# Attention scores in pairs of query tiles, with the last of five passes on half of the tensor engine's rows

## The chip, the cores and the metric

The kernel runs on one core of one Trainium2 chip. The metric is the device time in microseconds (us) of one execution, from the launch on the chip to its end; lower is better. "PE" is TensorE's matmul stream and "PEld" its weight loads, "DVE" is VectorE, "ACT" ScalarE, "POOL" GpSimd and "SP" SyncE, whose queue issues nearly all DMAs.

## The reference: what is computed

A sequence of 1024 tokens of width 1024 passes through two layers and a final RMSNorm. Layer 0 is causal attention with low-rank q and kv projections, layer 1 a gated convolution. The change touches layer 0 only, and in it the scores of the 8 heads:

```python
q_nope, q_pe = jnp.split(q, [QK_NOPE], axis=-1)       # 128 and 64 wide per head
k_nope, v = jnp.split(kv, [QK_NOPE], axis=-1)
q_pe = apply_rope(q_pe, cos[:, :, None, :], sin[:, :, None, :])
k_pe = apply_rope(k_pe, cos, sin)                     # one k_pe, shared by all heads
q = jnp.concatenate([q_nope, q_pe], axis=-1)
...
s = jnp.einsum('bqhd,bkhd->bhqk', qi, kf) * scale     # + causal mask, softmax, times v
```

A score is thus a sum over 128 plain and 64 rotary channels.

## The kernel before, in words

All matmuls that matter here run on operands of the 32-bit format fp32r, which holds fewer mantissa bits than fp32. Each operand is therefore split into a rounded part (suffix h) and the rest (suffix l), and a product takes several passes that add into the same PSUM tile: high x high, high x low, low x high.

The attention stage runs head by head. `proj(h)` loads the head's rotary part `rq` by four DMAs and its gate, and makes `qh`, `ql`, `kh`, `kl` (tiles `pj`) and, every second head, the values (`pv`). `score(h, i)` makes the scores of query tile i (128 queries) against all keys up to it, in chunks of 256 to 512 columns, in a PSUM tile `S`; there are two such tiles in rotation. Each chunk takes five passes (lines 538 to 542): three over the 128 plain channels, and two with `rq` as weights over the rotary channels. `rq` holds 128 rows: the two 32-row halves of the rounded rotary q (kinds 0 and 1), and below them the two halves of its rest (kinds 2 and 3). `krh` and `krl` hold the rotary k's rounded part and rest, each of them twice, in rows 0 to 63 and again in rows 64 to 127. So the fourth pass (`krh`) adds high x high and low x high at once, and the fifth (`krl`) adds high x low, and low x low. After the five passes the mask is added and the row maximum taken on DVE (lines 545, 546), the exponential on ACT (548), and the division by the row sum on POOL (551); this gives the tile `P`. `attend(h, c)` transposes `P` on PE (tiles `T`, line 564), splits it on ACT and DVE (`pth`, `ptl`) and multiplies with the values into `po`.

The order in which instructions stand on each engine in this stage is set by a scheduler at build time, which goes by the order of the program text as a priority, by free tiles, and by its own estimate of times. On the chip each engine runs its instructions in that order. The first part of the program (up to about 182 us) has a PE order written out by hand.

Of the kernel before, what the change touches and what calls it, by code (L numbers as in the profile page):

```python
# [9 lines left out]
F32 = mybir.dt.float32  # L10
# [3 lines left out]
AF = mybir.ActivationFunctionType  # L14
ALU = mybir.AluOpType
AX = mybir.AxisListType
PSUM = bass.MemoryType.PSUM

P = 128
T = 1024  # L20
# [5 lines left out]
CH = 512  # L26
# [38 lines left out]
def hybrid_body(ctx, tc, xT, xP, pos, cols, w1a, w1b, wqr, wqk, wv, wo, wc, we, out):  # L65
    nc = tc.nc
    v, s, g, pe, sp = nc.vector, nc.scalar, nc.gpsimd, nc.tensor, nc.sync
# [18 lines left out]
    for a in range(1, 4):  # L86
# [4 lines left out]
    ropeS = [[tc.dram_tile([P, T], F32, name=f"ropeS{k}{p_}") for p_ in range(2)]  # L91
             for k in range(4)]
# [5 lines left out]
    def load_w(src, n, nm, alloc=None, eng=None):  # L98
        if alloc is None:
            def alloc(name):  # L100
                return wp.tile([P, 1024], F32R, tag="w", bufs=5, name=name)
        raw = wp.tile([P, 1024], F32, tag="wraw", name=f"wr_{nm}")
        sp.dma_start(raw[:, :n], src)
        hi = alloc(f"wh_{nm}")
        s.activation(hi[:, :n], raw[:, :n], AF.Copy)
        lo = alloc(f"wl_{nm}")
        (eng or early_eng[0]).tensor_tensor(lo[:, :n], raw[:, :n], hi[:, :n].bitcast(F32), ALU.subtract)  # L107
        return hi, lo
# [4 lines left out]
    def split_early(src, nm):  # L113
        raw = wp.tile([P, 1024], F32, tag="wraw", name=f"sr_{nm}")
        sp.dma_start(raw, src)
        hi = wp.tile([P, 1024], F32R, tag="w", bufs=5, name=f"sh_{nm}")
        lo = wp.tile([P, 1024], F32R, tag="w", bufs=5, name=f"sl_{nm}")
        for a in range(2):
            cs = sl(a, CH)
            s.activation(hi[:, cs], raw[:, cs], AF.Copy)  # L120
            early_eng[0].tensor_tensor(lo[:, cs], raw[:, cs], hi[:, cs].bitcast(F32), ALU.subtract)
        loS[nm] = tc.dram_tile([P, 1024], F32, name=f"loS{nm}")
        sp.dma_start(loS[nm], lo.bitcast(F32))
# [13 lines left out]
    def mm3(ps, wh, wl, xh, xl, start, stop):  # L137
        pe.matmul(ps, wh, xh, start=start, stop=False)  # L138
        pe.matmul(ps, wh, xl, start=False, stop=False)  # L139
        pe.matmul(ps, wl, xh, start=False, stop=stop)  # L140
# [67 lines left out]
    def sl(k, n=P):  # L208
        return slice(k * n, (k + 1) * n)
# [9 lines left out]
    krh = midk.tile([P, T], F32R, name="krh")  # L219
    krl = midk.tile([P, T], F32R, name="krl")  # L220
# [187 lines left out]
    for a in range(4):  # L408
        b = a ^ 1
# [51 lines left out]
    b1 = es_b.enter_context(tc.tile_pool(name="b1", bufs=1, reuse_waits="tile"))  # L461
    psS_p = es_b.enter_context(tc.tile_pool(name="psS", bufs=2, space=PSUM, reuse_waits="tile"))
# [3 lines left out]
    mask = b1.tile([P, P], F32, name="mask")  # L466
# [8 lines left out]

    def proj(h):
        rq = b2.tile([P, T], F32R, tag="rq", name=f"rq{h}")
        for kind in range(4):
            sp.dma_start(rq[32 * kind : 32 * kind + 32, :].bitcast(F32),
                         ropeS[kind][h // 4][32 * (h % 4) : 32 * (h % 4) + 32, :])  # L480
        gt = b2.tile([P, T], F32, tag="gate", name=f"gateB{h}")
        sp.dma_start(gt, gateS[h])
        wh, wl = load_w(wqk[h], 640, f"qk{h}")
        q_h = b2.tile([P, T], F32R, tag="qh", name=f"qh{h}")
        q_l = b2.tile([P, T], F32R, tag="ql", name=f"ql{h}")
        k_h = b2.tile([P, T], F32R, tag="kh", name=f"kh{h}")
        k_l = b2.tile([P, T], F32R, tag="kl", name=f"kl{h}")
        for dst_h, dst_l, sh_, sl_, n, off, scale in (
            (q_h, q_l, qnh, qnl, NQL, 0, QSCALE),
            (k_h, k_l, kvh, kvl, NKV, NQL, 1.0),  # L490
        ):
            for c in range(2):
                ch = sl(c, CH)
                ps = psA_p.tile([P, CH], F32, tag="acc", name=f"pj{h}{off}{c}")
                for k in range(n):
                    mm3(ps, wh[:, sl(off + k)], wl[:, sl(off + k)], sh_[k][:, ch], sl_[k][:, ch],
                        k == 0, k == n - 1)
                s.activation(dst_h[:, ch], ps, AF.Copy, scale=scale)
                v.scalar_tensor_tensor(dst_l[:, ch], ps, scale, dst_h[:, ch].bitcast(F32),
                                       ALU.mult, ALU.subtract)  # L500
        if h % 2 == 0:
            wh, wl = load_w(wv[h // 2], 512, f"v{h}")
            vh = b2.tile([P, KD, 256], F32R, tag="vh", name=f"vh{h}")
            vl = b2.tile([P, KD, 256], F32R, tag="vl", name=f"vl{h}")
            for t2 in range(KD // 2):
                ps = psA_p.tile([P, CH], F32, tag="acc", name=f"pv{h}{t2}")
                for a in range(2):
                    tk = sl(2 * t2 + a)
                    for k in range(NKV):
                        pa_ = ps[:, sl(a, 256)]  # L510
                        w_h, w_l = wh[:, sl(k, 256)], wl[:, sl(k, 256)]
                        pe.matmul(pa_, kvh[k][:, tk], w_h, start=(k == 0), stop=False)
                        pe.matmul(pa_, kvl[k][:, tk], w_h, start=False, stop=False)
                        pe.matmul(pa_, kvh[k][:, tk], w_l, start=False, stop=(k == NKV - 1))
                dh = vh[:, 2 * t2 : 2 * t2 + 2, :].rearrange("p a b -> p (a b)")
                dl = vl[:, 2 * t2 : 2 * t2 + 2, :].rearrange("p a b -> p (a b)")
                s.activation(dh, ps, AF.Copy)
                v.tensor_tensor(dl, ps, dh.bitcast(F32), ALU.subtract)
            vpair[h // 2] = (vh, vl)
        heads[h] = (q_h, q_l, k_h, k_l, rq, gt)  # L520

    probs = {}

    def score(h, i):
        q_h, q_l, k_h, k_l, rq, _ = heads[h]
        nk = (i + 1) * P
        ps = psS_p.tile([P, T], F32, tag="S", name=f"S{h}_{i}")
        if i == 0:
            chunks, off = [(0, 256)], 0
        elif i == 4:  # L530
            chunks, off = [(0, 384), (384, 640)], 128
        else:
            chunks, off = [(a, min(a + CH, nk)) for a in range(0, nk, CH)], 0
        qs = sl(i)
        for a, b in chunks:
            o_ = ps[:, off + a : off + b]
            ks = slice(a, b)
            pe.matmul(o_, q_h[:, qs], k_h[:, ks], start=True, stop=False)
            pe.matmul(o_, q_h[:, qs], k_l[:, ks], start=False, stop=False)
            pe.matmul(o_, q_l[:, qs], k_h[:, ks], start=False, stop=False)  # L540
            pe.matmul(o_, rq[:, qs], krh[:, ks], start=False, stop=False)
            pe.matmul(o_, rq[:, qs], krl[:, ks], start=False, stop=True)
        st = b1.tile([P, 3], F32, tag="st", bufs=8, name=f"st{h}_{i}")
        last = ps[:, off + i * P : off + nk]
        v.tensor_tensor(last, last, mask, ALU.add)
        v.tensor_reduce(st[:, 0:1], ps[:, off : off + nk], AX.X, ALU.max, negate=True)  # L546
        pr = b1.tile([P, nk], F32, tag=f"P{i}", bufs=2 if i in (2, 3) else 1, name=f"P{h}_{i}")
        s.activation(pr[:, :nk], ps[:, off : off + nk], AF.Exp, bias=st[:, 0:1],  # L548
                     accum_out=st[:, 1:2])
        v.reciprocal(st[:, 2:3], st[:, 1:2])  # L550
        g.tensor_scalar(pr[:, :nk], pr[:, :nk], st[:, 2:3], 1.0, ALU.mult, ALU.mult)  # L551
        probs[h, i] = pr

    def attend(h, c, dst=None):
        vh, vl = vpair[h // 2]
# [48 lines left out]

    ogt = {}
    proj(0)
    pending = None
    for h in range(NH):
        for i in range(8):
            score(h, i)  # L610
            if i == 1 and pending is not None:
                attend(*pending)
                pending = None
            if i == 3 and h + 1 < NH:
                proj(h + 1)
            if i == 4 and h < 2:
                split_early(wc[22 + h], f"cg{6 + h}")
            if i == 6:
                split_early(we[h], f"e{h}")
            if i == 5:  # L620
                if h < NH - 1:
                    attend(h, 0)
                else:
                    ogt[0] = [load_og("A", h_, 0) for h_ in range(NH - 1)]
                    ogt[0].append(act_tile("A", f"og0{h}"))
                    attend(h, 0, ogt[0][h])
        pending = (h, 1)
# [499 lines left out]
```

## Time and profile before

| what | value |
|---|---|
| time, median of 3 runs | 908.65 us (908.37 to 911.29) |
| profiled execution | 909.12 us, of which span from first to last instruction 907.2 us |
| PE busy | 894.3 us (99%) of the span, 4432 matmuls |
| PEld, DVE, ACT, POOL busy | 82%, 72%, 56%, 41% |
| attention stage | about 182 to 424 us of the span |

The span is what the profiler saw between the first and the last instruction; the profiled execution's own time is 1.92 us longer. A busy PE is one that has at least one matmul on its way; since matmuls are pipelined, what one matmul costs is the distance from its start to the next one's start, not its recorded duration.

### The profile page before, as it was taken

The page shows a single profiled execution, that of the slowest core. Times are in us where ns is not written, and L with a number is a line of the kernel's source. Part 1 is how long each engine was busy: PE and PEld are TensorE (multiplying, and loading weights), DVE is VectorE, ACT ScalarE, POOL GpSimd, SP SyncE. Part 2 cuts the span into 40 slices and gives each one's busy share as a digit, 9 for nine tenths or more (in the row PEclk, how much of TensorE's full clock was granted, in tenths as well). Part 3 has the DMA queues.
Part 4 walks back from the last instruction along what each step waited for, and adds up shares of the span by engine and source line. Part 5 has one row for each costly group of instructions (what it writes and reads, how often), then busy time and mean ns, then how long its engine had stood idle before and what let it go on. Part 6 is the DMA issues. An engine that isn't in the chain of part 4 may idle for free.

```text
span 907.2 us, 12407 instructions
## 1 busy us (share of the span) xinstructions
PE 894.3 (99%) x4432; PEld 745.0 (82%) x4432; DVE 650.4 (72%) x1108; ACT 504.4 (56%) x839; POOL 370.6 (41%) x335
## 2 busy tenths in 40 slices
PE   9999999999999999999999999999999999999996
PEld 7888888888888988978887878888888887778996
DVE  7668957647656666676464958999999997687543
ACT  8435454255555554574343447766666773678732
POOL 0000000143442532642234559999999993000034
PEclk9999999999999999999999999999999999999998
DMA  7223644563332331551364411111112223145714
GB/s 269 93 71 128 221 159 167 224 200 117 121 107 85 120 106 49 185 179 54 111 232 127 154 57 47 48 47 46 47 48 95 93 92 109 54 139 186 267 60 145
DMA packets 39677, 110.18 MB, mean 121 GB/s; under 512 B 5248, under 2 KB 8320, under 8 KB 39616
## 3 DMA queue, kind: packets, MB, share of 16 engines
q1 hardware_dynamic: 39248, 108.74, 36.0%
q8 instruction: 35, 0.57, 0.3%
q10 hardware_dynamic: 288, 0.39, 0.1%
q14 instruction: 26, 0.21, 0.1%
q0 software_dynamic: 80, 0.26, 0.1%
HBM read 83.93 MB, written 24.92 MB: 120 GB/s over the span
## 4 chain that ended last, share of the span: by engine, by line
PE 90%; DMA 3%; DVE 2%; ACT 2%; POOL 1%; issue 1%; SPq 1%; DVEq 0%; ACTq 0%; POOLq 0%
PE ps_b L138 5%; PE ps_b L140 5%; PE ps_b L139 5%; PE cb L139 3%; PE cb L140 3%; PE cb L138 3%; PE cg L138 3%; PE cg L139 3%; PE cg L140 3%; PE e L138 3%; PE e L140 3%; PE e L139 3%; PE T L564 3%; PE ca L138 3%; PE ca L140 3%; PE ca L139 3%
## 5 line engine op out<-in xcount | busy, mean ns | idle before, releaser
L816 POOL TENSOR_TENSOR dcv<-dcv,pkb 128x512 f32<-128x512 f32 (+1 forms) x126 | 157.8, 1255 | 8.5 <-ACT pkb L815 1.0
L815 ACT ACTIVATE pkb<-u,taps 128x512 f32<-128x512 f32 (+1 forms) x126 | 83.6, 674 | 55.9 <-POOL dcv L816 51.2
L551 POOL TENSOR_SCALAR P<-P,st 128x128 f32<-128x128 f32 (+3 forms) x64 | 48.1, 753 | 121.9 <-DVE st L550 114.4
L827 DVE SCALAR_TENSOR_TENSOR av<-u,taps,av 128x512 f32<-128x512 f32 (+1 forms) x135 | 91.8, 688 | 1.2 <-ACT av L821 1.1
L107 POOL TENSOR_TENSOR wl_qk<-wr_qk,wh_qk 128x640 fp32r<-128x640 f32 x8 | 12.6, 1571 | 174.3 <-PE ps_b L139 167.7
L829 DVE SCALAR_TENSOR_TENSOR cv<-su,gsum,cv 128x512 f32<-128x512 f32 (+1 forms) x117 | 80.6, 689 | 0.4
L574 DVE TENSOR_TENSOR ptl<-T,pth 128x512 fp32r<-128x512 f32 (+1 forms) x96 | 52.3, 554 | 30.9 <-ACT pth L573 30.5
L573 ACT ACTIVATE pth<-T 128x512 fp32r<-128x512 f32 (+1 forms) x96 | 46.0, 490 | 50.5 <-PE T L564 44.1
L138 PE MATMUL ps_b<-xgh,wh_b 128*128 128x512 f32 x176 | 69.9, 397 | 0.0
L140 PE MATMUL ps_b<-xgh,wl_b 128*128 128x512 f32 x176 | 69.6, 395 | 0.0
L139 PE MATMUL ps_b<-xgl,wh_b 128*128 128x512 f32 x176 | 69.6, 395 | 0.0
L1006 POOL TENSOR_TENSOR x<-x,rbe 128x512 f32<-128x512 f32 (+1 forms) x16 | 16.2, 1045 | 126.7 <-DMA rbe<-rowe 121.5
L107 POOL TENSOR_TENSOR wl_o<-wr_o,wh_o 128x1024 fp32r<-128x1024 f32 x16 | 41.5, 2596 | 55.4 <-PE o L140 21.8
L138 PE MATMUL e<-a_y,wh_e 128*128 128x256 f32 (+1 forms) x192 | 61.7, 322 | 0.0
L140 PE MATMUL e<-a_y,wl_e 128*128 128x256 f32 (+1 forms) x192 | 61.5, 320 | 0.0
L139 PE MATMUL e<-a_y,wh_e 128*128 128x256 f32 (+1 forms) x192 | 61.4, 320 | 0.0
L548 ACT ACTIVATE P<-S,st 128x128 f32<-128x128 f32 (+3 forms) x64 | 47.4, 741 | 24.2 <-DVE st L546 17.6
L138 PE MATMUL cg<-a_h,wh_cg 128*128 128x512 f32 x128 | 51.7, 404 | 0.0
L139 PE MATMUL cb<-a_h,wh_cb 128*128 128x512 f32 x128 | 50.8, 397 | 0.8 <-DVE a_h L746 0.8
L140 PE MATMUL o<-a_og,wl_o 128*128 128x512 f32 x128 | 51.0, 398 | 0.3 <-POOL wl_o L107 0.3
L138 PE MATMUL o<-a_og,wh_o 128*128 128x512 f32 x128 | 51.0, 400 | 0.1
L138 PE MATMUL ca<-a_h,wh_ca 128*128 128x512 f32 x128 | 50.8, 397 | 0.0
(321 smaller groups left out, 2679.8 us busy)
## 6 DMA issues: line engine op xcount, KB each, us to landing
wr_o<-in_wo_dram SPq DMA_DIRECT2D x16, 512.0 KB, 4.0
wr_e<-in_we_dram SPq DMA_DIRECT2D x14, 512.0 KB, 4.7
wl_e<-loSe SPq DMA_DIRECT2D x14, 512.0 KB, 4.0
wr_b<-in_w1b_dram SPq DMA_DIRECT2D x11, 512.0 KB, 3.3
sr_cg<-in_wc_dram SPq DMA_DIRECT2D x8, 512.0 KB, 4.5
loScg<-sl_cg SPq DMA_DIRECT2D x8, 512.0 KB, 2.9
gateS<-gt SPq DMA_DIRECT2D x8, 512.0 KB, 4.7
rq<-ropeS SPq DMA_DIRECT2D x32, 128.0 KB, 3.4
```

Source lines behind the costliest of these rows:

```text
L107: (eng or early_eng[0]).tensor_tensor(lo[:, :n], raw[:, :n], hi[:, :n].bitcast(F32), ALU.subtract)
L138: pe.matmul(ps, wh, xh, start=start, stop=False)
L139: pe.matmul(ps, wh, xl, start=False, stop=False)
L140: pe.matmul(ps, wl, xh, start=False, stop=stop)
L548: s.activation(pr[:, :nk], ps[:, off : off + nk], AF.Exp, bias=st[:, 0:1], accum_out=st[:, 1:2])
L551: g.tensor_scalar(pr[:, :nk], pr[:, :nk], st[:, 2:3], 1.0, ALU.mult, ALU.mult)
L573: s.activation(hi[:, n0:], pt[:, n0:], AF.Copy)
L574: v.tensor_tensor(lo[:, n0:], pt[:, n0:], hi[:, n0:].bitcast(F32), ALU.subtract)
L815: s.activation(pk, lag(src, i), AF.Copy, scale=tap(of, i))
L816: g.tensor_tensor(acc, acc, pk, ALU.add)
L827: v.scalar_tensor_tensor(a_, lag(E, i), tap(dwe, i), a_, ALU.mult, ALU.add)
L829: v.scalar_tensor_tensor(c_, lag(su, i), tap(gsum, i), c_, ALU.mult, ALU.add)
```

## The change

`score(h, i)` becomes `score_pair(h, i0)`, which is called for every even i and writes two score tiles. For each of the two tiles it writes passes one to four of all chunks; then come the fifth passes of both tiles, chunk by chunk in turn; then the softmax of both. The fifth pass uses 64 rows instead of 128: rows 0 to 63 for even query tiles and rows 64 to 127 for odd ones (`tile_position=(r0, 0)`), so that the two passes of a pair stand in different halves of the array. For this the rounded rotary q must lie in the upper rows for even query tiles and in the lower rows for odd ones: each of the four DMAs of `rq` is cut in two, one for the even and one for the odd blocks of 128 tokens, with the kinds turned by two for the odd ones. The fifth pass now adds high x low alone; the product low x low is left out.

```diff
     def proj(h):
         rq = b2.tile([P, T], F32R, tag="rq", name=f"rq{h}")
+
+        def alt(ap, b):
+            return ap.rearrange("p (i b n) -> p i b n", b=2, n=P)[:, :, b, :]
+
         for kind in range(4):
-            sp.dma_start(rq[32 * kind : 32 * kind + 32, :].bitcast(F32),
-                         ropeS[kind][h // 4][32 * (h % 4) : 32 * (h % 4) + 32, :])
+            for b in range(2):
+                at = 32 * ((kind + 2 * b) % 4)
+                sp.dma_start(alt(rq[at : at + 32, :].bitcast(F32), b),
+                             alt(ropeS[kind][h // 4][32 * (h % 4) : 32 * (h % 4) + 32, :], b))
...
-    def score(h, i):
+    def score_pair(h, i0):
         q_h, q_l, k_h, k_l, rq, _ = heads[h]
...
+        pss, todo = {}, {}
+        for i in (i0, i0 + 1):
...
+            for a, b in chunks:
+                o_ = ps[:, off + a : off + b]
+                ks = slice(a, b)
+                pe.matmul(o_, q_h[:, qs], k_h[:, ks], start=True, stop=False)
+                pe.matmul(o_, q_h[:, qs], k_l[:, ks], start=False, stop=False)
+                pe.matmul(o_, q_l[:, qs], k_h[:, ks], start=False, stop=False)
+                pe.matmul(o_, rq[:, qs], krh[:, ks], start=False, stop=False)
+                todo[i].append((o_, qs, ks))
+            pss[i] = ps, off, nk
+
+        for j in range(max(len(x_) for x_ in todo.values())):
+            for i in (i0, i0 + 1):
+                if j < len(todo[i]):
+                    o_, qs, ks = todo[i][j]
+                    r0 = 64 * (i % 2)
+                    pe.matmul(o_, rq[r0 : r0 + 64, qs], krl[r0 : r0 + 64, ks],
+                              start=False, stop=True, tile_position=(r0, 0))
...
         for i in range(8):
-            score(h, i)
+            if i % 2 == 0:
+                score_pair(h, i)
```

The scheduler turns this text into an order. Three places show what it makes of it. The first is PE in head 0, at the pair of tiles 2 and 3 (`S_2`, `S_3`; line 542 before and line 559 after are the fifth pass; `pv` and `T` are other work). Before:

```order
L538 MATMUL S_2_1660<-kh_1522,qh_1520 128x384
L539 MATMUL S_2_1660<-kl_1523,qh_1520 128x384
L540 MATMUL S_2_1660<-kh_1522,ql_1521 128x384
L541 MATMUL S_2_1660<-krh,rq_1507 128x384
L542 MATMUL S_2_1660<-krl,rq_1507 128x384
L564 MATMUL T_1792<-ident,P_0_1643 128x128
L538 MATMUL S_3_1673<-kh_1522,qh_1520 128x512
L539 MATMUL S_3_1673<-kl_1523,qh_1520 128x512
L540 MATMUL S_3_1673<-kh_1522,ql_1521 128x512
L541 MATMUL S_3_1673<-krh,rq_1507 128x512
L542 MATMUL S_3_1673<-krl,rq_1507 128x512
```

After the change:

```order
L547 MATMUL S_2_1664<-kh_1526,qh_1524 128x384
L548 MATMUL S_2_1664<-kl_1527,qh_1524 128x384
L549 MATMUL S_2_1664<-kh_1526,ql_1525 128x384
L550 MATMUL S_2_1664<-krh,rq_1507 128x384
L559 MATMUL S_2_1664<-krl,rq_1507 128x384
L584 MATMUL T_1800<-ident,P_0_1653 128x128
L547 MATMUL S_3_1669<-kh_1526,qh_1524 128x512
L548 MATMUL S_3_1669<-kl_1527,qh_1524 128x512
L549 MATMUL S_3_1669<-kh_1526,ql_1525 128x512
L550 MATMUL S_3_1669<-krh,rq_1507 128x512
L559 MATMUL S_3_1669<-krl,rq_1507 128x512
```

Nothing moved here: a transpose and four full passes stand between the fifth pass of tile 2 and that of tile 3. The second place is PE in head 4, at tiles 4 and 5, one of the few where the fifth passes of two tiles became neighbours (`po` is the product with the values). Before:

```order
L541 MATMUL S_4_3249<-krh,rq_2785 128x256
L542 MATMUL S_4_3249<-krl,rq_2785 128x256
L538 MATMUL S_5_3267<-kh_2800,qh_2798 128x512
L539 MATMUL S_5_3267<-kl_2801,qh_2798 128x512
L540 MATMUL S_5_3267<-kh_2800,ql_2799 128x512
L541 MATMUL S_5_3267<-krh,rq_2785 128x512
L542 MATMUL S_5_3267<-krl,rq_2785 128x512
```

After the change:

```order
L550 MATMUL S_5_3282<-krh,rq_2801 128x256
L559 MATMUL S_4_3273<-krl,rq_2801 128x384
L559 MATMUL S_5_3282<-krl,rq_2801 128x512
L559 MATMUL S_4_3273<-krl,rq_2801 128x256
L138 MATMUL po_3088<-pth_3094,vh_2110 128x512
L559 MATMUL S_5_3282<-krl,rq_2801 128x256
L139 MATMUL po_3088<-ptl_3095,vh_2110 128x512
```

Here three fifth passes follow each other in alternating halves, and a fourth stands alone. Over the whole program the 96 fifth passes stand in 63 groups of neighbours with other work between the groups; in 4 of the groups passes of both halves meet, and the others hold one pass, or two of the same tile and so of the same half. The third place is the SP queue at the start of the stage, where `rq` of head 0 is loaded. Before:

```order
L479 DMA rq_1507<-ropeS_81 32x1024
L479 DMA rq_1507<-ropeS_83 32x1024
L479 DMA rq_1507<-ropeS_85 32x1024
L479 DMA rq_1507<-ropeS_87 32x1024
L482 DMA gateB_1512<-gateS_89 128x1024
```

After the change:

```order
L485 DMA rq_1507<-ropeS_81 32x4x128 x2
L485 DMA rq_1507<-ropeS_83 32x4x128 x2
L485 DMA rq_1507<-ropeS_85 32x4x128 x2
L485 DMA rq_1507<-ropeS_87 32x4x128 x2
L488 DMA gateB_1516<-gateS_89 128x1024
```

Four issues of 32 rows of 4 KB became eight of 32 rows of four 512-byte pieces, ahead of the gate's load.

## Rows read from the trace of the kernel before

**Rows 1.** The page: busy time of each engine, and PE's granted clock in 40 slices.

```profile
PE 894.3 (99%) x4432; PEld 745.0 (82%) x4432; DVE 650.4 (72%) x1108; ACT 504.4 (56%) x839; POOL 370.6 (41%) x335
...
PEclk9999999999999999999999999999999999999998
```

**Rows 2.** Busy time by stage, in us; the middle stretch is the attention stage.

```profile
182.00:424.00 242.00, 240.43 (x1402) 209.57 (x1401) 155.27 (x341) 136.81 (x298) 95.00 (x124) 1.00 0.39 124
```

**Rows 3.** PE's waits from 182 to 425 us: total, times, longest.

```profile
PE po L139 <- DVE ptl L574: 0.9, 3, 0.5
PE S L538 <- ACT P L548: 0.3, 1, 0.3
PE S L541 <- DMA rq<-ropeS: 0.2, 1, 0.2
```

**Rows 4.** Groups by line and shape: the fifth pass, busy us and mean ns.

```profile
L542 PE MATMUL S<-krl,rq 128*128 128x512 f32 x40 | 16.0, 400 | 0.0
...
L542 PE MATMUL S<-krl,rq 128*128 128x256 f32 x32 | 9.0, 281 | 0.0
...
L542 PE MATMUL S<-krl,rq 128*128 128x384 f32 x24 | 8.1, 336 | 0.0
```

**Rows 5.** Timeline, head 7: start, duration in us; passes and their weight loads.

```profile
413.91 0.40 PE L542 MATMUL S<-krl,rq 128*128 128x512 f32 x1
413.91 0.19 PEld L538 LDWEIGHTS S<-kh,qh 128*128 128x128 f32 x1
414.14 0.28 PE L538 MATMUL S<-kh,qh 128*128 128x256 f32 x1
414.15 0.19 PEld L539 LDWEIGHTS S<-kl,qh 128*128 128x128 f32 x1
414.26 0.28 PE L539 MATMUL S<-kl,qh 128*128 128x256 f32 x1
```

**Rows 6.** Timeline, head 7: passes of 384 columns.

```profile
407.00 0.33 PE L541 MATMUL S<-krh,rq 128*128 128x384 f32 x1
407.00 0.19 PEld L542 LDWEIGHTS S<-krl,rq 128*128 128x128 f32 x1
...
407.17 0.34 PE L542 MATMUL S<-krl,rq 128*128 128x384 f32 x1
```

**Rows 7.** Timeline, head 0: a pass whose weights were loaded late.

```profile
185.93 0.19 PEld L138 LDWEIGHTS pj<-kvh,wh_qk 128*128 128x128 f32 x1 [0.45 <-DVE ql L499]
185.93 0.51 PE L138 MATMUL pj<-kvh,wh_qk 128*128 128x512 f32 x1
...
186.28 0.39 PE L139 MATMUL pj<-kvl,wh_qk 128*128 128x512 f32 x1
```

**Rows 8.** Timeline, head 7: a change from transposes to matmuls.

```profile
412.08 0.39 PE L140 MATMUL po<-pth,vl 128*128 128x512 f32 x1
...
412.31 0.60 PE L564 MATMUL T<-ident,P 128*128 128x128 f32 x4
...
412.64 0.19 PEld L138 LDWEIGHTS po<-pth,vh 128*128 128x128 f32 x1
412.67 0.48 PE L138 MATMUL po<-pth,vh 128*128 128x512 f32 x1
...
412.99 0.39 PE L538 MATMUL S<-kh,qh 128*128 128x512 f32 x1
```

**Rows 9.** Timeline of the SP queue, heads 0 and 1: DMA issues.

```profile
182.53 2.81 SPq L479 DMA_DIRECT2D rq<-ropeS  x4
185.39 0.42 SPq L482 DMA_DIRECT2D gateB<-gateS  x1
```

**Rows 10.** The tile rq: its issues in ns, its way to landing.

```profile
L479 SPq DMA_DIRECT2D rq<-ropeS x32: 302/416/1580, 182.5 to 367.2; - x32
...
DMA to landing us min/median/max: 2.1/3.4/6.1
```

**Rows 11.** Timeline of PE, head 0: the first pass that reads rq.

```profile
189.68 0.36 PE L541 MATMUL S<-krh,rq 128*128 128x256 f32 x1 [0.17 <-DMA rq<-ropeS]
```

**Rows 12.** DVE's waits from 182 to 424 us: total, times, longest.

```profile
DVE st L550 <- ACT P L548: 20.3, 30, 2.8
DVE S L545 <- PE S L542: 19.8, 25, 2.1
DVE ptl L574 <- ACT pth L573: 16.8, 34, 1.6
```

More of the change, by code (lines that the diff above doesn't have):

```diff
@@ L522, in hybrid_body @@
     probs = {}
-    def score(h, i):
+    def score_pair(h, i0):
         q_h, q_l, k_h, k_l, rq, _ = heads[h]
[L526 to L552, printed above, removed]
@@ new lines, in score_pair @@
+        pss, todo = {}, {}
+        for i in (i0, i0 + 1):
+            nk = (i + 1) * P
+            ps = psS_p.tile([P, T], F32, tag="S", name=f"S{h}_{i}")
+            if i == 0:
+                chunks, off = [(0, 256)], 0
+            elif i == 4:
+                chunks, off = [(0, 384), (384, 640)], 128
+            else:
+                chunks, off = [(a, min(a + CH, nk)) for a in range(0, nk, CH)], 0
+            qs = sl(i)
+            todo[i] = []
+            for a, b in chunks:
[7 more added lines that the diff above has]
+            pss[i] = ps, off, nk
@@ new lines, in score_pair @@
+        for j in range(max(len(x_) for x_ in todo.values())):
[5 more added lines that the diff above has]
+                              start=False, stop=True, tile_position=(r0, 0))
+        for i in (i0, i0 + 1):
+            ps, off, nk = pss[i]
+            st = b1.tile([P, 3], F32, tag="st", bufs=8, name=f"st{h}_{i}")
+            last = ps[:, off + i * P : off + nk]
+            v.tensor_tensor(last, last, mask, ALU.add)
+            v.tensor_reduce(st[:, 0:1], ps[:, off : off + nk], AX.X, ALU.max, negate=True)
+            pr = b1.tile([P, nk], F32, tag=f"P{i}", bufs=2 if i in (2, 3) else 1, name=f"P{h}_{i}")
+            s.activation(pr[:, :nk], ps[:, off : off + nk], AF.Exp, bias=st[:, 0:1],
+                         accum_out=st[:, 1:2])
+            v.reciprocal(st[:, 2:3], st[:, 1:2])
+            g.tensor_scalar(pr[:, :nk], pr[:, :nk], st[:, 2:3], 1.0, ALU.mult, ALU.mult)
+            probs[h, i] = pr
```

## The prediction, made before the changed kernel had run

> **What bounds the kernel now.** I read the page first: PE is busy for 894.3 of 907.2 us, the next engine for 72%, and the granted clock is at its upper level (2.4 GHz) in every slice [rows 1]. So the program is as long as PE's row of matmuls. Next the table by stage: the change lies in the attention stage, where PE is busy for 240.4 of 242.0 us with the clock at 1.00 [rows 2]. Third, PE's waits there: 0.9, 0.3 and 0.2 us, 1.4 us together [rows 3]. Two things follow. Nothing that the change does on other engines can give more than these 1.4 us. And whatever it adds to or takes from PE's row comes out in the time one to one.
>
> The unit is then the distance between the starts of neighbouring passes. It is 0.23 us for 512 columns and 0.12 for 256 [rows 5], and 0.17 for 384 [rows 6]; the recorded 0.40, 0.28 and 0.34 hold a tail of about 0.165 us in which the next pass is already running. The reader should also see when weights are loaded: the load of the next pass starts with the pass before it (413.91 and 413.91, 414.14 and 414.15) [rows 5]. So a load costs nothing as long as it may run beside a pass.
>
> **The change part by part.** *What it is worth if two fifth passes share the array.* There are 40, 24 and 32 fifth passes of 512, 384 and 256 columns [rows 4]. At the distances above that is 9.2 + 4.1 + 3.8 = 17.1 us of PE's row. Each head has six pairs of partners; the shorter of each has 256 columns twice, 384 three times, 512 once: 0.24 + 0.52 + 0.23 = 0.98 us a head, 7.9 us in all. That is the most that running side by side can give.
>
> *What the order leaves of it.* PE runs in the order shown in the section on the change. A full pass needs all rows, so only fifth passes that are neighbours can overlap. Of 48 pairs, 5 stand so (three borders of 256 columns, two of 384): 3 x 0.12 + 2 x 0.17 = 0.7 us. The reason is visible at tiles 2 and 3: the second tile waits for its PSUM buffer or its turn, and the scheduler puts the first tile's fifth pass where it stood before. I take -0.7 us, bounds 0 and -0.7.
>
> *What it adds: changes of the array's shape.* The 96 fifth passes stand in 63 groups with 128-row work on both sides. So PE goes 126 times between 128-row and 64-row passes; before, never. No row of the trace before shows such a change, so I bound its price. From below: nothing. The nearest row for that is the change from transposes to matmuls: four transposes start at 412.31, the matmul at 412.67, the one after at 412.99 [rows 8]. The fourth transpose's own start is about 0.03 us ahead of the matmul, so the two together last about 0.35 us, against 0.11 + 0.23 = 0.34 for the same pieces apart (a transpose takes 0.11: four of them between 412.31 and 412.67, less that 0.03). That change of mode is nearly free. But it leaves all 128 rows in one piece. From above: the old pass must leave the array entirely, its tail of 0.165 us, and only then are the new weights loaded, unhidden. An unhidden load has a row: the pass at 185.93 starts with its load instead of after it, lasts 0.51 instead of 0.39, and holds the next start off by 0.35 instead of 0.23 us, 0.12 more [rows 7]; after transposes a late load costs 0.48 against 0.39 or 0.32 against 0.23, 0.09 more [rows 8]. The upper bound is 0.165 + 0.12 = 0.285 us a change.
>
> Between 0 and 0.285 I take 0.12: a load for rows in another grouping cannot run beside a pass that uses them all, but the pass itself needs no more than its columns to get out of the way. 126 x 0.12 = 15.1 us; the bounds are 0 and 35.9 us.
>
> The Trainium skill speaks against this change, in "TensorEngine Tiling (Array Packing)", Key Properties: changing the tiling mode, not just the tile, drains TensorE. No run here shows it yet; its price would be the upper bound, if draining includes the load, and the tail alone, 126 x 0.165 = 20.8 us, if not.
> On the other side "TensorE: Matmul & The Clock Gate", Part 3, says that a weight load is pulled ahead of running matmuls when it meets other row groups or the spare weight buffer; the loads above agree for equal shapes, and if it holds across shapes, the lower bound is right.
>
> *The loads of rq.* Four issues became eight. An issue takes 0.42 us in the middle [rows 10], so the last one of head 0 goes out 4 x 0.42 = 1.7 us later than in the 2.81 us before [rows 9], that is starts near 186.6. From issue to landing it is 2.1 to 6.1 us, mostly 3.4 [rows 10]: landing at 188.7 to 192.7, mostly 190.0. PE's first reader stands at 189.68 and waited 0.17 us already [rows 11]. Behind it in PE's row all else waits. So 0 to 3.0 us; I take 0.5. The bytes are the same, the pieces are 512 bytes instead of 4 KB; that more pieces take longer is in the bound. The gate's load behind them on SP moves by the same 1.7 us and is not needed before head 0's `po` ends. Later heads load `rq` a head ahead (the last at 367.2 for head 7 [rows 10], whose passes stand at 407 and on [rows 6]): hidden; it would cost as here if the cover went.
>
> *The softmax.* Mask and maximum of a tile come after its fifth pass. Where that moved (S_4 in head 4 goes behind eight passes of S_5, some 1.4 us), DVE gets S_4 later, and `P` and its transposes after it. DVE waits 19.8 us for the scores already, and is busy for 155 of 242 us [rows 12, 2]; PE has other work of the next head to run in between. I take 0, bounds -1.4 (all waits of PE gone) and +2.
>
> *Sum.* Against the profiled execution's own 909.12 us: + 15.1 + 0.5 - 0.7 = 924.0. That execution is 0.47 us above the median of 908.65, so I forecast 923.5 us, 1.6% slower.
>
> **The rivals.** *Changes of shape are free* (up to 0.02 us each, 2.5 us). For it speaks that weights go in beside a running pass and that the change from transposes costs about 0.01 us [rows 5, 8]; against it, that neither row changes the grouping of rows. Then 908.65 - 0.7 + 0.5 = 908.5, up to 911. This is the rival on the other side, not slower; it decides below 0.02 us a change.
>
> *The array empties and then loads*: 126 x 0.285 = 35.9, 909.12 + 35.9 - 0.2 - 0.47 = 944.4 us; with the tail alone 929.3. [...] Against it: nothing in the trace before makes a matmul wait for the end of the one before. By the rule of the Trainium skill on changing the tiling mode ("TensorEngine Tiling (Array Packing)", Key Properties) it would come out so.
>
> *The halves overlap as the change is written*: 908.65 - 7.9 + 0.5 = 901.3 us. Against it stands the order. It would need shape changes that are free as well.
>
> *A late rq alone*: a chip queue that takes eight issues badly (one of 32 took 1.58 us [rows 10]) stalls head 0 by 3 us: 911.5 with free changes. It adds to each other case and is in the ends of the range.
>
> **How the numbers follow.** A difference of 0.3% (2.7 us) is about what a measurement of this kernel can tell from none. Chances: changes cost 0.02 to 0.165 us each (911 to 929.3, the forecast's own range) 0.43; more than that, up to and past the full emptying, 0.25; free, 0.27; a gain of over 2.7 us 0.05. So faster 0.05, same 0.27, slower 0.68. The range takes in the free case and the full emptying: 908 to 945 us; outside it I leave about 0.06 below and 0.08 above.
>
> **What would show it.** In the changed profile PE's row should be as before outside the fifth passes. Right: the distance from a fifth pass to the pass after it, and from the pass before to it, is longer than 0.23, 0.17 or 0.12 us by 0.1 on average, the weight load of each 64-row pass starts after, not with, the pass before it, and the attention stage is about 15 us longer while the stages around it are unchanged. Free changes: the same distances as before. Emptying: the next start at the end of the recorded tail or later. For the overlap: at tiles 4 and 5 of head 4, two starts within a few hundredths of a us of each other. For `rq`: PE's wait for the DMA in head 0 grows from 0.17 us. I am wrong if the fifth passes are shorter than their columns, or if PE's waits for `pth`, `ptl` or `S` in the stage grow past 2 us.

## The result, and the profile after

The change made the kernel slower: 935.3 us in the median (933.95 to 937.01) against 909.87 us for the kernel before, run beside it (908.37 to 911.29). The ratio is 1.028, with a 95% interval of 1.026 to 1.030. That is 25.4 us more, where 15 had been forecast. The profiled execution of the changed kernel took 934.02 us, its span is 931.9 us, 24.7 us more than before.

The page of the changed kernel, in the two parts that stand for the kernel before in [rows 1]:

```profile
PE 917.9 (98%) x4432; PEld 745.0 (80%) x4432; DVE 655.0 (70%) x1108; ACT 503.8 (54%) x839; POOL 368.3 (40%) x335
...
PEclk9999999999999999999999999999999999999998
```

PE executes as many matmuls as before, at the same granted clock, and is busy for 23.6 us more. The busy time by stage of the changed kernel says where (from:to, length, then busy time of PE, PEld, DVE, ACT and POOL, granted clock, DMA share, GB/s):

```profile
0.00:182.00 182.00, 180.95 (x777) 146.49 (x778) 130.10 (x181) 89.16 (x118) 4.01 (x10) 1.00 0.48 166
182.00:449.00 267.00, 264.30 (x1408) 209.34 (x1408) 158.77 (x342) 136.65 (x298) 95.36 (x123) 1.00 0.35 112
449.00:931.90 482.90, 472.63 (x2250) 389.18 (x2248) 366.15 (x586) 278.00 (x423) 268.97 (x202) 0.99 0.31 103
```

The attention stage has grown from 242 us [rows 2] to 267. The stages around it are as long as before (482.9 us behind it, 483.2 before). PE's waits in that stage, changed kernel (total, times, longest; to be read against [rows 3]):

```profile
PE S L547 <- ACT P L568: 2.0, 2, 1.6
PE po L139 <- DVE ptl L594: 0.2, 1, 0.2
```

They are 2.2 us now and were 1.4. So of 24.7 us only 0.8 are waits for other engines; the rest must stand between neighbouring passes of PE's own row. The groups by shape show it first at the fifth pass, which streams exactly the columns it streamed before [rows 4]:

```profile
L559 PE MATMUL S<-krl,rq 64*128 64x512 f32 x40 | 17.7, 475 | 0.0
L559 PEld LDWEIGHTS S<-krl,rq 64*128 64x128 f32 x96 | 14.7, 184 | 14.3 <-issue 10.8
L559 PE MATMUL S<-krl,rq 64*128 64x256 f32 x32 | 10.1, 335 | 0.0
L559 PE MATMUL S<-krl,rq 64*128 64x384 f32 x24 | 9.8, 407 | 0.0
```

Each is 0.05 to 0.08 us longer in the record, and PEld sits idle for 14.3 us ahead of its weights, most of it put down to "issue", that is to nothing that another engine does. In the kernel before it was 1.8 us:

```profile
L542 PEld LDWEIGHTS S<-krl,rq 128*128 128x128 f32 x96 | 18.0, 188 | 1.8
```

The timeline of PE in head 0 gives the price (start, duration in us):

```profile
195.87 0.40 PE L550 MATMUL S<-krh,rq 128*128 128x512 f32 x1
196.20 0.50 PE L559 MATMUL S<-krl,rq 64*128 64x512 f32 x1
196.62 0.39 PE L518 MATMUL pv<-wh_v,kvh 128*128 128x256 f32 x1
196.85 0.28 PE L519 MATMUL pv<-wh_v,kvl 128*128 128x256 f32 x1
```

Three distances are longer than those of [rows 5]. From the last 128-row pass to the 64-row pass it is 0.33 us instead of 0.23: 0.09 to 0.10 more. From there to the next 128-row pass it is 0.42 instead of 0.23: 0.19 more. And that pass of 256 columns holds its successor off by 0.23 instead of 0.12: 0.11 more. The weight loads explain the pattern. The same change of shape at a pass of 384 columns, with PEld:

```profile
194.19 0.35 PE L549 MATMUL S<-kh,ql 128*128 128x384 f32 x1
194.20 0.19 PEld L550 LDWEIGHTS S<-krh,rq 128*128 128x128 f32 x1
...
194.38 0.34 PE L550 MATMUL S<-krh,rq 128*128 128x384 f32 x1
...
194.65 0.18 PEld L559 LDWEIGHTS S<-krl,rq 64*128 64x128 f32 x1 [0.26 <-issue]
194.65 0.44 PE L559 MATMUL S<-krl,rq 64*128 64x384 f32 x1
...
195.02 0.14 PEld L584 LDWEIGHTS T<-ident,P 128*128 128x128 f32 x1 [0.19 <-issue]
195.02 0.33 PE L584 MATMUL T<-ident,P 128*128 128x128 f32 x1
```

Between passes of one shape the load starts with the pass before (194.20 beside 194.19). Across a change it starts with its own pass (194.65 and 194.65, 195.02 and 195.02), and that start is late: 0.27 us after the fourth pass instead of 0.17, 0.37 after the fifth. A change of shape thus costs a gap of about 0.09 us ahead of the pass, in which no new pass starts (called emptying here; the recorded end of the 128-row pass at 195.87 is 0.07 us after the next start, and ends are modelled, so the record does not show when the array is empty), and about 0.105 us behind it, because its load was not hidden: 0.195 us together, or 0.39 for a group of fifth passes, which has two changes.

Added up over the stage, each distance less 0.231, 0.172, 0.118 or 0.108 us for 512, 384, 256 or 128 columns: the 63 changes into a group cost 6.3 us (median 0.092), the 63 changes out of one 9.6 us (median 0.190), the first 128-row passes after a group 5.9 us (median 0.105), 28 neighbouring 64-row passes 3.0 us (25 of them stand in one half, about 0.107 each: the group's own unhidden load), and five neighbours in different halves give back 0.74 us. That is 24.1 of the 24.7 us.

### The profile page after: what moved, and what is told of

The parts are those of the page before. It is cut to its first block, busy times and chain, and to the rows that moved or that the text cites. A ratio compares the mean times of both kernels' runs of the same rounds, so it can differ in the third digit from the quotient of the medians.

```text
span 931.9 us, 12460 instructions
## 1 busy us (share of the span) xinstructions
PE 917.9 (98%) x4432; PEld 745.0 (80%) x4432; DVE 655.0 (70%) x1108; ACT 503.8 (54%) x839; POOL 368.3 (40%) x335
## 4 chain that ended last, share of the span: by engine, by line
PE 93%; DVE 2%; ACT 2%; DMA 1%; POOL 1%; SPq 1%; issue 0%; DVEq 0%; ACTq 0%; POOLq 0%
PE ps_b L138 4%; PE ps_b L139 4%; PE ps_b L140 4%; PE T L584 3%; PE cb L139 3%; PE cb L140 3%; PE cb L138 3%; PE cg L138 3%; PE cg L139 3%; PE cg L140 3%; PE ca L140 3%; PE ca L138 3%; PE ca L139 3%; PE S L559 3%; PE e L138 3%; PE e L140 3%
## 5 line engine op out<-in xcount | busy, mean ns | idle before, releaser
L107 POOL TENSOR_TENSOR wl_o<-wr_o,wh_o 128x1024 fp32r<-128x1024 f32 x16 | 39.6, 2481 | 63.0 <-PE o L140 30.1
```

## The experiments

Three questions are told apart: is it the shape that costs, and which part of it; what would running side by side give if the order allowed it; and what do the pairing and the eight DMAs do by themselves. In the table "changes" are changes between 128-row and 64-row passes, "account" is the sum over distances as above (with what overlap gives back) in the profiled execution, and the difference is between medians. The profiled execution was the longest of the four for neighbours_two_halves (929.49 us), pair_full_rows (923.44) and half_rows_tile_end (938.1).

| kernel | changes | account, us | median, us | before beside it, us | difference, us | ratio (95%) |
|---|---|---|---|---|---|---|
| the change | 126 | 24.1 | 935.3 | 909.87 | +25.4 | 1.028 (1.026 to 1.030) |
| half_rows_unpaired | 192 | 37.2 | 944.53 | 909.47 | +35.1 | 1.0385 (1.037 to 1.040) |
| half_rows_tile_end | 130 | 26.3 | 936.48 | 909.66 | +26.8 | 1.0293 (1.028 to 1.031) |
| rows96_whole_array | 0 | | 910.28 | 909.47 | +0.8 | 1.0015 (1.0005 to 1.003) |
| neighbours_one_half | 64 | 12.3 | 929.66 | 909.66 | +20.0 | 1.0223 (1.021 to 1.024) |
| neighbours_two_halves | 64 | 5.4 | 925.5 | 909.47 | +16.0 | 1.0188 (1.016 to 1.021) |
| neighbours_four_dmas | 64 | 4.5 | 923.29 | 908.77 | +14.5 | 1.0165 (1.015 to 1.018) |
| change_four_dmas | 124 | 23.4 | 932.68 | 908.77 | +23.9 | 1.0265 (1.025 to 1.028) |
| pair_full_rows | 0 | | 920.16 | 909.47 | +10.7 | 1.0116 (1.010 to 1.013) |
| pair_full_rows_four_dmas | 0 | | 914.33 | 909.66 | +4.7 | 1.0057 (1.004 to 1.007) |
| rq_eight_dmas_alone | 0 | | 915.56 | 909.66 | +5.9 | 1.0066 (1.005 to 1.009) |
| no_fifth_pass | 0 | | 897.31 | 908.77 | −11.5 | 0.9873 (0.986 to 0.989) |

**The shape alone: half_rows_unpaired.** The kernel before, with its order and its four DMAs, and the fifth pass on 64 rows; low x low is left out, as in the change. Each of the 96 fifth passes is then a group of its own. In the trace PE goes through the same sequence of tiles and widths as before.

```diff
-            pe.matmul(o_, rq[:, qs], krl[:, ks], start=False, stop=True)
+            pe.matmul(o_, rq[:64, qs], krl[:64, ks], start=False, stop=True,
+                      tile_position=(0, 0))
```

> The kernel before with one edit: the fifth pass uses rows 0 to 63, with no pairing and rq loaded as before; the product low x low is left out. Its 96 fifth passes stand in 96 groups, none beside another, so the shape changes 192 times. Theory of the array's shape: 192 x 0.195 = 37.4 us, 910 + 37 = 947 us. Rival (a 64-row pass is slower by itself, 24.7 us over 96 passes, whatever stands beside it): 935 us.

Measured: 944.53 us, as the theory of a price per change expects (192 x 0.195 = 37.4 us; the account has 37.2, and PE's waits in the stage became a little shorter). The groups of this kernel:

```profile
L542 PE MATMUL S<-krl,rq 64*128 64x512 f32 x40 | 19.8, 494 | 0.0
...
L542 PEld LDWEIGHTS S<-krl,rq 64*128 64x128 f32 x96 | 17.5, 183 | 24.8 <-issue 20.8
```

Nothing is paired here and no DMA is added, and the fifth pass and PEld's idle time look as in the change, more of both. So the change of shape alone costs more than the whole edit did.

**The same with fewer changes: half_rows_tile_end.** As before it, but a tile's fifth passes are written together after its four other passes of all chunks.

```diff
-            pe.matmul(o_, rq[:, qs], krl[:, ks], start=False, stop=True)
+        for a, b in chunks:
+            pe.matmul(ps[:, off + a : off + b], rq[:64, qs], krl[:64, a:b], start=False,
+                      stop=True, tile_position=(0, 0))
```

> The unpaired kernel with 64-row fifth passes, but the fifth passes of a tile's two chunks stand together at its end: 65 groups instead of 96. Theory of the array's shape: 130 changes x 0.195 = 25.4 us, 909.5 + 25.4 = 935 us, about 2 us less if PE's old waits vanish beside them as in the run with 192 changes (944.5 us measured, 947 computed). Rival (a price per 64-row pass): 944.5 us, as with 96 groups.

Measured: 936.48 us with 65 groups. With 130 changes instead of 192 the account falls by 10.9 us and the time by 8.1 (PE's waits for an exponential, 2.0 us, are new here as they are in the change). It takes as long as the changed kernel, which has 126 changes: 1.0293 and 1.028, with intervals that overlap. What counts is the number of changes, not the number of 64-row passes.

**Rows, or the array in pieces: rows96_whole_array.** The kernel before, with the fifth pass on 96 rows; half of low x low is left out.

```diff
-            pe.matmul(o_, rq[:, qs], krl[:, ks], start=False, stop=True)
+            pe.matmul(o_, rq[:96, qs], krl[:96, ks], start=False, stop=True)
```

> The kernel before with one edit: the fifth pass uses 96 of the 128 rows, which keeps the array in one piece (tile of 128 x 128); half of the product low x low is left out. Theory of the array's shape: no change, 908 to 912 us. Rival (a change in the number of rows in use is what costs): 947 us, as 96 passes on 64 rows would.

Measured: 910.28 us, 0.15% more than before. The groups:

```profile
L542 PEld LDWEIGHTS S<-krl,rq 96*128 96x128 f32 x95 | 17.9, 188 | 1.7
...
L542 PE MATMUL S<-krl,rq 96*128 96x512 f32 x39 | 15.8, 404 | 0.0
```

PEld has 1.7 us of idle time, as before the change (1.8), instead of 24.8. Using 96 of 128 rows costs next to nothing; using a half of the array between passes that use all of it does. No run used 64 rows without `tile_position`, so which of the two, the number of rows or the position, makes the change of shape is not told apart.

**What running side by side gives: neighbours_two_halves and neighbours_one_half.** In both the fifth passes of a pair are held together behind its last fourth pass, which leaves 32 groups, one for each pair. In the first the two tiles use different halves; in the second both use rows 0 to 63, and `rq` is loaded by four DMAs as before.

```diff
-                pe.matmul(o_, rq[:, qs], krh[:, ks], start=False, stop=False)
+                last4 = pe.matmul(o_, rq[:, qs], krh[:, ks], start=False, stop=False)
...
+        with tc.issue_after(last4.ins), tc.high_priority():
             for j in range(max(len(x_) for x_ in todo.values())):
...
-                    r0 = 64 * (i % 2)
+                    r0 = 0      # in neighbours_one_half only
```

> The change with the order forced: the fifth passes of both tiles of a pair are held behind the last fourth pass of the second tile and given the highest priority, so that they stand in 32 groups, all of them alternating between the halves. Theory of the array's shape: 64 changes x 0.195 = 12.5 us, less 7.9 us of columns that run side by side: 910 + 4.6 = 914.5 us, somewhat more if PE then waits for the softmax. Rival (halves do not overlap, the 3 ns between starts are only the queue's): 910 + 12.5 = 922.5 us. Rival (per pass): 935 us.

> The forced neighbours (32 groups) with all fifth passes in the upper half, and rq loaded by four DMAs. Theory (halves run side by side): the 7.2 us that overlap gave come back, so about 7 us slower than the same kernel with two halves (925.5), 932 us, less whatever the four saved DMAs a head give. Rival (the 3 ns between starts hide a later wait, halves do not overlap): 925 us or less.

Measured: 925.5 and 929.66 us. The first is far above the time expected (914.5) and even above 922.5, the rival without overlap, so the time alone does not show overlap; the distances between passes do. The second is 2.3 us below 932, from which the saved DMAs were still to come off. The timeline of PE has the fifth passes of tiles 2 and 3, 384 and 512 columns, in two halves:

```profile
196.32 0.39 PE L550 MATMUL S<-krh,rq 128*128 128x512 f32 x1
196.64 0.49 PE L560 MATMUL S<-krl,rq 64*128 64x384 f32 x2
197.06 0.39 PE L518 MATMUL pv<-wh_v,kvh 128*128 128x256 f32 x1
```

From the start of the two to the next pass it is 0.42 us, as much as the 512 columns alone took at 196.20 in the changed kernel: the 384 columns cost nothing. In one half, in neighbours_one_half, two passes of the same sizes, in head 1:

```profile
223.87 0.66 PE L558 MATMUL S<-krl,rq 64*128 64x384 f32 x2
224.46 0.50 PE L138 MATMUL po<-pth,vh 128*128 128x512 f32 x1
```

Here it is 0.59 us, longer by the 0.17 of 384 columns. So overlap is real, and over all pairs it is worth 12.3 − 5.4 = 6.9 us of the account. These two kernels also differ in the DMAs of `rq`. The cleaner pair is neighbours_one_half and neighbours_four_dmas (below): both load `rq` by four DMAs, and between them the halves are worth 12.3 − 4.5 = 7.8 us of the account and 20.0 − 14.5 = 5.5 us of time. The forced order nevertheless does not pay: 64 changes cost 12.5 us by the price above, and 10.6 of the 16.0 us of neighbours_two_halves are not in the account at all. They are partly in PE's idle time (9.1 us from 182 to 445 us; before, 1.6 in the stage [rows 2]) and clock. PE's largest waits in that kernel from 182 to 440 us, and the start of the stage:

```profile
PE S L547 <- ACT P L569: 4.2, 7, 1.4
PE po L138 <- ACT pth L594: 2.3, 1, 2.3
```

```profile
182.00:250.00 68.00, 64.97 (x342) 52.26 (x341) 35.11 (x77) 32.95 (x71) 23.31 (x31) 0.95 0.35 110
```

PE idles for 3.0 of these 68 us, and the clock is 0.95; in neighbours_one_half it is 1.00 over the stage.

**The pairing and the DMAs alone: pair_full_rows, pair_full_rows_four_dmas, rq_eight_dmas_alone.** The first is the change with the fifth pass on 128 rows, the second the same with `rq` loaded as before. The third is the kernel before with the change's eight DMAs for each `rq` (half of the columns of `rq` then have their kinds exchanged, which leaves the sum over its 128 rows as it was).

```diff
-                    pe.matmul(o_, rq[r0 : r0 + 64, qs], krl[r0 : r0 + 64, ks],
-                              start=False, stop=True, tile_position=(r0, 0))
+                    pe.matmul(o_, rq[:, qs], krl[:, ks], start=False, stop=True)
```

> The change with one edit: the fifth passes use all 128 rows again; text, order of the passes (the same 63 groups), the eight DMAs of rq and the softmax in pairs stay. Theory of the array's shape (each of the 126 changes between 128-row and 64-row passes costs 0.09 us of emptying and 0.105 us of unhidden weight load): there are no changes left, so the time of before, 908 to 912 us. Rival (the pairing is to blame: late softmax, smaller DMA pieces): the time stays near 935 us.

> The pairing with 128-row fifth passes, and rq loaded by four DMAs in the layout of before. The pairing with 128 rows and eight DMAs took 920.2 us against 909.5, with 9.7 us of PE waits in the attention stage. Theory (the eight issues of rq on SP hold back other loads that ACT waits for, with the softmax queued behind them): 908 to 912 us. Rival (the order that the pairing gives the passes and the softmax makes the waits): 918 to 922 us.

> The kernel before with only the eight DMAs of rq and its alternating layout; unpaired, the fifth passes on 128 rows, and the same order on PE, DVE and POOL as before. Theory (the eight issues make waits): 913 to 921 us. Rival (the order of the pairing makes them): 909 to 911 us, with a wait for rq in head 0 of up to 1 us.

Measured: 920.16, 914.33 and 915.56 us. The third is as expected. The second lies between its two expectations, and the first between its own: taking the shape out gives 15 us back, not 25. What stays is a stretch of waits, in the stage table and in PE's waits of pair_full_rows:

```profile
182.00:439.00 257.00, 246.75 (x1411) 213.33 (x1410) 156.39 (x342) 136.00 (x299) 95.73 (x124) 0.99 0.36 117
```

```profile
PE S L547 <- ACT P L566: 5.4, 6, 1.6
PE po L138 <- ACT pth L591: 3.1, 2, 2.1
PE po L139 <- DVE ptl L592: 1.2, 4, 0.6
```

PE idles for 10.3 us of the stage (before: 1.6 [rows 2]). Where it idles most, the clock falls too. The stage table of the same kernel from 250 to 280 us:

```profile
250.00:280.00 30.00, 26.70 (x139) 22.65 (x139) 14.27 (x30) 13.70 (x28) 10.39 (x12) 0.94 0.34 111
```

PE is idle for 3.3 us of these 30, and the granted clock is 0.94 in the mean, so partly at the lower of its two levels. The kernel before has 1.00 here:

```profile
250.00:280.00 30.00, 29.97 (x171) 25.86 (x170) 19.04 (x41) 17.75 (x38) 12.74 (x16) 1.00 0.40 131
```

Some of the loss is that. One place shows what the exponential waits for, on ACT of pair_full_rows:

```profile
211.42 1.16 ACT L120 ACTIVATE sh_cg<-sr_cg 128x512 fp32r<-128x512 f32 x2 [0.78 <-DMA sr_cg<-in_wc_dram]
212.48 0.99 ACT L566 ACTIVATE P<-S,st 128x896 f32<-128x896 f32 x1
```

The exponential (L566) stands behind a conversion of the next layer's weights that waits for its own DMA; before, the same conversion starts at 210.50 without a wait. The next wait of PE is for the exponential after this one, which itself waits for its maximum from DVE; how much of it goes back to the late conversion was not traced:

```profile
216.05 1.12 ACT L566 ACTIVATE P<-S,st 128x1024 f32<-128x1024 f32 x1 [2.05 <-DVE st L564]
217.31 0.38 PE L547 MATMUL S<-kh,qh 128*128 128x256 f32 x1 [1.44 <-ACT P L566]
```

The pairing's order costs 4.7 us and the eight DMAs 5.9 us, each alone; the sum, 10.6, is what both cost together, 10.7. Here the two simply add.

**The DMAs in the change: change_four_dmas and neighbours_four_dmas.** The alternating layout is written into the DRAM tensor `ropeS` in the first part of the program, once, and each head loads `rq` by four DMAs.

```diff
-            sp.dma_start(ropeS[j][pr], hi.bitcast(F32))
-            sp.dma_start(ropeS[2 + j][pr], t2)
+            for b in range(2):
+                sp.dma_start(alt(ropeS[(j + 2 * b) % 4][pr], b), alt(hi.bitcast(F32), b))
+                sp.dma_start(alt(ropeS[(2 + j + 2 * b) % 4][pr], b), alt(t2, b))
...
-            for b in range(2):
-                at = 32 * ((kind + 2 * b) % 4)
-                sp.dma_start(alt(rq[at : at + 32, :].bitcast(F32), b),
-                             alt(ropeS[kind][h // 4][32 * (h % 4) : 32 * (h % 4) + 32, :], b))
+            sp.dma_start(rq[32 * kind : 32 * kind + 32, :].bitcast(F32),
+                         ropeS[kind][h // 4][32 * (h % 4) : 32 * (h % 4) + 32, :])
```

> The change as it is, but the alternating layout of rq is made where the rotary q is stored in the first stage, so that each head's rq is again loaded by four DMAs of 4 KB rows; the order on PE is that of the change (62 groups). Theory (the gaps of the shape changes already hide what the eight DMAs cost): 933 to 936 us, as the change. Rival (prices add up; the eight DMAs alone cost 5.9 us): 929 to 930 us.

> The forced neighbours in two halves (32 groups, 925.5 us measured), with rq loaded by four DMAs in the alternating layout. By the account of that run 5.4 us of its 16 us are shape changes less overlap; the rest are waits, which here have fewer gaps to hide in. Theory (of these, the eight DMAs make 5 to 6 us, the order of the pairing 5): 919 to 921 us. Rival (the DMAs are hidden here too): 925 us. In both cases slower than before.

Measured: 932.68 us, ratio 1.0265 against the change's 1.028, with intervals that overlap; and 923.29 us, 1.0165 against 1.0188. In the change the eight DMAs are thus nearly free (1.5 us between the differences). In the forced order taking them out gives 1.5 to 2 us, less than the 5.9 of rq_eight_dmas_alone; these intervals overlap too, so it is not told from nothing. PE's waits for the exponentials stay (neighbours_four_dmas):

```profile
PE S L545 <- ACT P L567: 4.3, 8, 1.4
```

**The most that there is to win: no_fifth_pass.** The kernel before without its fifth pass; high x low of the rotary part is left out.

> The kernel before without the fifth pass; the product high x low of the rotary channels is left out. Theory (PE's row is the time, one to one): 17.1 us less, 892.5 us, up to 3 us more if waits for the softmax come to light. Rival (the attention stage is bound by the softmax on DVE and ACT): 900 us or more.

Measured: 897.31 us, 11.5 us less, of 17.1 that the passes take in PE's row; that is between the two expectations. Of the rest 2.4 us are idle time of PE in the stage (4.0 us from 182 to 424 us after 1.6, in waits for `pth`, `ptl`, `P` and `kh` mostly), and 1.1 us a longer wait at the very end of the program (`bce` for `rte`, 2.4 us after 1.3). What remains of it was not traced. In this order even a free fifth pass would give no more than the 11.5 us.

## Why the prediction was right in direction and short in size

**The bound.** Right. What is added to PE's row came out in the time: the account of 24.1 us and 0.8 us of waits make up the 24.7 us by which the span grew, all of it in the attention stage. One reading was loose: the last slice of PEclk in [rows 1] is an 8, so the clock is at its upper level in every slice but the last, which lies behind the stage.

**The order and the overlap.** Right. Of 48 pairs five stand as neighbours and run side by side; −0.7 us was expected and −0.74 measured. At tiles 4 and 5 of head 6 the two halves' passes start 4 ns apart, and four passes of 384, 512, 256 and 256 columns (0.64 us of columns) occupy PE from 401.98 to 402.53:

```profile
401.98 0.61 PE L559 MATMUL S<-krl,rq 64*128 64x384 f32 x4
402.53 0.19 PEld L138 LDWEIGHTS po<-pth,vh 128*128 128x128 f32 x1 [0.25 <-issue]
402.53 0.50 PE L138 MATMUL po<-pth,vh 128*128 128x512 f32 x1
```

**The price of a change of shape: the step that failed.** The count, 126, was right. The term "126 x 0.12 = 15.1 us" was mis-sized: a change measured 0.195 us, 24.6 us in all. The prediction held two prices against each other, the unhidden load, 0.12, and the load behind a full emptying, 0.165 + 0.12 = 0.285, and took the load alone, because "the pass itself needs no more than its columns to get out of the way". The runs show that it needs more, and less than the recorded tail: the next start is 0.09 us late at 512, 384 and 256 columns alike, and the load adds 0.105 us behind it. Both parts are there, and neither end was right. The emptying, which the choice put at nothing, adds 126 x 0.09 = 11.3 us, and the load, 0.105 instead of 0.12, takes 1.9 back. The time lies inside the stated 908 to 945 us, but the prediction's own price range, 0.02 to 0.165 us, with a chance of 0.43, misses 0.195, which falls to the case that it gave 0.25. Two of its signs came out otherwise: the 5.9 us on the first 128-row pass after a group lie outside the fifth passes, where PE's row was to be as before; and PE's waits for `S` and `ptl` in the stage come to 2.2 us, past the 2 us at which it called itself wrong, though they are only 1.0 more than before. A bound made of a modelled tail (0.165 us) was too high by 0.07; the late load in [rows 7], 0.12, was a good row for its part.

The rule of the Trainium skill on changing the tiling mode ("TensorEngine Tiling (Array Packing)", Key Properties) is that TensorE drains. The trace agrees as far as it goes: 0.09 us without a new start, and the load behind it.

The Trainium skill says that a load is pulled ahead of running matmuls when it meets other row groups or the spare weight buffer ("TensorE: Matmul & The Clock Gate", Part 3). The trace agrees within one shape (194.19 and 194.20). Across two shapes the loads are not pulled ahead (194.65 and 194.65), so the reading by which the lower bound would be right is out.

The rivals were 944.4 us for emptying and load, and 908.5 us for free changes; the time lies between, nearer to the first, with its mechanism and a smaller emptying. The nearest number of all, 929.3 us for the tail alone, has no unhidden load in it, so that nearness is chance.

**The loads of rq.** The forecast of 0.5 us was about right for the changed kernel. The eight issues of head 0 take 5.69 us instead of 2.81, a median of 0.60 us each instead of 0.42, more than was assumed; the first reader waited 0.3 us (before 0.17):

```profile
182.35 5.69 SPq L485 DMA_DIRECT2D rq<-ropeS  x8
188.09 0.59 SPq L488 DMA_DIRECT2D gateB<-gateS  x1
```

The medians over all heads come from the changed kernel's tile `rq` (to be read against [rows 10]):

```profile
L485 SPq DMA_DIRECT2D rq<-ropeS x64: 538/597/1640, 182.3 to 390.6; - x64
```

But the argument was thin. "Hidden", for the later heads, fails without the changes of shape: there the eight DMAs cost 5.9 us (rq_eight_dmas_alone). That the gaps of the changes cover them in the changed kernel fits these times and is not shown by a trace.

**The softmax.** Taken as 0, within −1.4 to +2; PE's waits rose by 0.8 us. Alone the pairing costs 4.7 us (pair_full_rows_four_dmas); here too the gaps would cover it, which again is argued from the times. That the 24.7 us in the change are the changes of shape and not these two is shown by half_rows_tile_end, which has neither the pairing nor the DMAs, and about as many changes, and the same time.

**Could it pay?** A group costs 0.39 us. The most that partners can share in one pair is 0.40 us (tiles 6 and 7), and 0.29, 0.17 and 0.12 in the others: 0.98 us a head against 4 x 0.39 = 1.56. By these numbers only the pair of tiles 6 and 7 would break even, so no order of the pairs can win in this kernel; that is worked out and was not run, and the best that ran is 1.0165 times the time before.

**What stays open.** Why the pairing's order and the eight issues each lengthen the waits for `P` and `pth` is traced at one place only (ACT's queue behind a weight's DMA), and neither what delayed that DMA nor how much of PE's wait comes of it is known. Why taking the DMAs out gives at most some 2 us in the forced order, where alone they cost 5.9, was not found. And the 10.6 us of neighbours_two_halves outside the account are placed by waits and clock only in part.

## What to carry to other kernels

Before packing two small matmuls into halves of the array, count in the order as it is built how often PE goes between whole-array and half-array passes: each such change cost 0.195 us here, so a group must share more than 0.39 us of columns (some 860 at the 0.23 us that 512 take) to gain anything. Look at the weight load beside the pass to see it: a load that starts with its own pass instead of with the one before is not hidden. And take a cost that is hidden behind gaps as hidden only as long as the gaps are there.

## What the runs showed that was not expected

Rows and shape are different things: 96 of 128 rows cost next to nothing (0.15%), a half of the array 35.1 us in the same order. The emptying is about the same after 512, 384 and 256 columns (medians 0.096, 0.090 and 0.092 us). Two halves start within 4 ns of each other and do not slow each other: 384 columns beside 512 were free. An issue on SP's queue that moves four pieces of 512 bytes for each of 32 rows takes 0.60 us, against 0.42 for one piece of 4 KB.
